# A hybrid RWKV/attention block on one core: the form of one low-rank product, the place of the state transposes, and the grouping of attention's value products

## The chip, the cores and the metric

The kernel runs on one core of one Trainium2 chip. The core has TensorE (matrix products, called PE in the profile, with its weight loads as PEld), VectorE (DVE), ScalarE (ACT), GpSimd (POOL) and SyncE (SP, which here issues DMAs). The metric is the device time of one launch in microseconds. The time before is 866.53 us, the median of three runs (866.11 to 867.91).

## What is computed

One residual block for 256 tokens of 2048 channels. The input is normalised, projected by one large matrix, run through two branches (an RWKV-7 time mixer and chunked attention, both 1024 wide with heads of 64), gated, merged, projected and normalised again. Cut to its core, the reference reads:

```python
h = _rms_norm(x, pre_norm_g[l])
proj = h @ w_in[l]
p_r, p_k, p_v, z_r, q_a, k_a_att, v_a, z_a, m_r, m_a = jnp.split(proj, split_points, axis=-1)
y_r = _rwkv7_mixer(h, p_r, p_k, p_v, ...) * jax.nn.silu(z_r)
y_a = _chunk_band_attention(q_a, k_a_att, v_a, rel_bias[l]) * jax.nn.silu(z_a)
u_r = y_r @ w_branch_rwkv[l]
u_a = y_a @ w_branch_attn[l]
merged = jax.nn.sigmoid(m_r + b_merge[l, 0]) * u_r + jax.nn.sigmoid(m_a + b_merge[l, 1]) * u_a
x = x + _rms_norm(merged @ w_out[l], post_norm_g[l])
```

In the time mixer, `a = sigmoid(a0 + (xa @ a1) @ a2)` is a low-rank product with an inner width of 64; its second layer, `@ a2`, is what the kernel calls `pa`. The state recurrence runs per head over the tokens:

```python
sa = einsum('bhvk,bhk->bhv', state, -kkt)
state = state * wt + sa * (kkt * at) + vt * kt
yt = einsum('bhvk,bhk->bhv', state, rt)
```

Attention is a softmax over the own chunk of 64 tokens and earlier ones, with a bias by relative position, followed by the product with the values.

## The kernel before

**Main products.** `run_plan` walks a list of large products (`k0`, `r0`, `v0`, the first low-rank layer, then `k`, `r`, `v`, `q`, `ak`, `zr`, `va`, `za` by column blocks, later the merge and the output). Each weight chunk is loaded by SyncE, split by ScalarE and VectorE into a high and a low part (`split`, lines 80 to 82), and multiplied in fp32r with accumulators `acc_...` in two wide PSUM buffers (pool `pm`, tag `mm`). An accumulator is free again when `done` has read it (`take`, lines 376 to 382).

**Side work.** Everything else is written as Python generators that are kept in two queues, `side` and `back`. After each chunk of a main product, `pump` takes a few steps of each: first `side`, then two of `back`. A step runs to the next `yield`. So the yields set the order in which the code asks for instructions and for buffers. The tile framework then schedules: it puts each engine's instructions in an order of its own, for which it simulates the engines, and gives out the buffers of each tag. Small results share four PSUM banks (`small`, pool `ps`, tag `sm`).

**The time mixer** handles 16 heads as eight tiles of 128 channels, two heads a tile. `duo_front(j0)` prepares two tiles (j0 is 0, 2, 4 or 6): decay sums `pc` (line 500), the low-rank `pa` (line 506), factors in `AB`, and products `pv` (546) and `pA` (553). Its 64 inner rows lie on partitions 64 to 127 of `za` and `RA`. `group_back(g)` works on four tiles (g is 0 or 1): it inverts small triangular blocks (`z`, `xx`, `x`), then runs a chain over four chunks c. In each chunk: `pw` (647, and 651 with the state `SB`), its copy `W` on ScalarE (653), the transposes `pt` (658) and their copy `BT` (659, not for the last chunk), `pu` (663) and its copies into `UV`, and after a yield `py` (672, 680), `pg` (677, from `BT` and `UV`), and the new state `SB` on VectorE (688, 690). The tag `BT` has two buffers, and `project_za` takes one of that tag for the gate `za2`.

**Attention.** `attend(j0)` handles two tiles: scores `pS` (822, 824), softmax, and then per tile the transposes `pT` of the probabilities (851) with their copies on ScalarE (853), a yield, the value products `po` (859, 862), the gate on VectorE (864) and a split into `ya`. `q`, `k` of the first two calls take buffers of the tags `k` and `r` that `duo_front` uses.

**Forms.** TensorE is addressed by rows and columns. The profile writes 128\*128 for the whole array, 64\*128 for half the rows (`pa`, `pA`, `pS`), 128\*64 for half the columns (`pv`, `pw`, `py`, `pg`, `po`), 64\*64 (`pu`, `z`, `xx`) and 32\*32. The main products, `pc`, `pt` and `pT` have the whole array. The list of buffers:

```python
pm = ctx.enter_context(tc.tile_pool(name="pm", bufs=2, space=PSUM))
ps = ctx.enter_context(tc.tile_pool(name="ps", bufs=4, space=PSUM))
```

Of the kernel before, what the change touches and what calls it, by code (L numbers as in the profile page):

```python
# [9 lines left out]
F32 = mybir.dt.float32  # L10
F32R = mybir.dt.float32r
AF = mybir.ActivationFunctionType
ALU = mybir.AluOpType
# [24 lines left out]
P = 128  # L38
D = 2048
DB = 1024  # L40
T = 256
C = 64
# [19 lines left out]
def kernel(ctx: ExitStack, tc, x, xt, vecs, w_in, wa1, w2, a2, w0, rel, w_br, w_ba, w_out, post_g, bm, out):  # L62
    nc = tc.nc
    PE, ACT, DVE, POOL = nc.tensor, nc.scalar, nc.vector, nc.gpsimd
# [4 lines left out]
    tp = ctx.enter_context(tc.tile_pool(name="tp", bufs=2))  # L69
# [4 lines left out]
    def small(name):  # L74
        return ps.tile([P, 512], F32, tag="sm", name=name)

    def col(t, o):
        return t[:, o:o + 1]
# [91 lines left out]
    ident = cp.tile([P, P], F32, name="ident")  # L170
# [193 lines left out]
    def normalise():  # L364
# [8 lines left out]
        RA.append(bg.tile([P, 2 * DB], F32, tag="R", name="RA"))  # L373
        nc.sync.dma_start(RA[0][64:128, DB:2 * DB], a2)

    def take(out, acc, raw=False):

        if raw:
            DVE.tensor_tensor(out, acc[:, :, 0:256], rb2, op=ALU.mult)
        else:  # L380
            ACT.activation(out, acc[:, :, 256:512], AF.Copy)
            DVE.tensor_tensor(out, acc[:, :, 0:256], out, op=ALU.add)
# [3 lines left out]
    RA = []  # L386
    zw = cp.tile([65, T], F32, name="zw")
    za = cp.tile([P, T], F32, name="za")
    POOL.memset(zw[64:65, :], 1.0)

    lab = []

    def lora_weights(q):
# [4 lines left out]
        else:  # L398
            lab.extend(bg.tile([P, 4, 256], F32, tag=t, name=f"lab_{t}") for t in ("Y", "s"))
        for g in (2 * q, 2 * q + 1):  # L400
# [31 lines left out]
    HS = (slice(0, 64), slice(64, 128))  # L432
# [33 lines left out]
    def duo_front(j0):  # L466
        g = j0 // 4
# [9 lines left out]
        AB, A, v, UV = d["AB"][q0 // 2], d["A"], d["v"], d["UV"]  # L477
# [19 lines left out]
        for m in range(2):  # L497
            pc = small(f"pc{j0}{m}")
            for i in range(2):
                PE.matmul(pc[:, i * 130:(i + 1) * 130], d["s"][:, i, (q0 + m) * P:(q0 + m + 1) * P],  # L500
                          cum.rearrange("p c t -> p (c t)"), start=True, stop=True)
            pcv = pc[:, 0:260].rearrange("p (c t) -> p c t", c=4)
            ACT.activation(pp[:, 4 * m:4 * m + 4, :], pcv, AF.Exp, scale=-DECAY)
            ACT.activation(iv[:, 4 * m:4 * m + 4, :], pcv[:, :, 1:65], AF.Exp, scale=DECAY)
            pa = small(f"pa{j0}{m}")
            PE.matmul(pa[:, :T], RA[0][64:128, DB + (j0 + m) * P:DB + (j0 + m + 1) * P], za[64:128, :], start=True, stop=True)
            ACT.activation(ta[:, m, :], pa[:, :T], AF.Tanh, scale=0.5, bias=col(hv, H_A0 + j0 + m))
            yield
        for m in range(2):
# [30 lines left out]
        for m in range(2):  # L540
            jj = q0 + m
# [22 lines left out]
    def group_back(g):  # L564
        d = G[g]
        AB, A, UV = d["AB"], d["A"], d["UV"]
# [17 lines left out]
        for i in range(14, -1, -1):  # L584
            n = 15 - i
# [50 lines left out]
        for q in range(2):  # L636
            ACT.activation(Rq[q][0:32, :, 32:64], p4[q][0:32, 0:256].rearrange("p (u t) -> p u t", u=8), AF.Copy)
            DVE.tensor_copy(Rq[q][64:96, :, 32:64], p4[q][64:96, 0:256].rearrange("p (u t) -> p u t", u=8))
        yield
        Y = bg.tile([P, 4, 4, C], F32, tag=("Y", "v")[g], name=f"Y{g}")  # L640
        d["Y"] = Y
        for c in range(4):
            pw = small(f"pw{g}{c}")
            for jj in range(4):
                for h in range(2):

                    PE.matmul(pw[HS[h], jj * C:(jj + 1) * C], A[:, h, jj, c, 0, :], UV[:, h, jj, c, :], start=jj == 0, stop=jj == 3 and not c)
            for jj in range(4):
                for h in range(2):
                    if c:  # L650
                        PE.matmul(pw[HS[h], jj * C:(jj + 1) * C], AB[jj // 2][:, jj % 2, c, 0, :], SB[:, jj, h, :], start=False, stop=jj == 3)
            W = tp.tile([P, 4, C], F32, tag="W", name=f"W{g}{c}", bufs=2)
            ACT.activation(W.rearrange("p j t -> p (j t)"), pw[:, 0:256], AF.Copy)
            if c < 3:
                BT = tp.tile([P, 4, P], F32, tag="BT", name=f"BT{g}{c}")
                pt = small(f"pt{g}{c}")
                for jj in range(4):
                    PE.transpose(pt[:, jj * P:(jj + 1) * P], AB[jj // 2][:, jj % 2, c, 2:4, :].rearrange("p a t -> p (a t)"), ident)
                ACT.activation(BT.rearrange("p j t -> p (j t)"), pt, AF.Copy)
            pu = small(f"pu{g}{c}")  # L660
            for jj in range(4):
                for h in range(2):
                    PE.matmul(pu[HS[h], jj * C:(jj + 1) * C], R[HS[h], jj * 4 + c, :], W[HS[h], jj, :], start=True, stop=True)
            puv = pu[:, 0:256].rearrange("p (j t) -> p j t", j=4)
            DVE.tensor_copy(UV[HS[0], 0, :, c], puv[HS[0]])
            ACT.activation(UV[HS[1], 1, :, c], puv[HS[1]], AF.Copy)
            yield
            py = small(f"py{g}{c}")
            for jj in range(4):
                for h in range(2):  # L670
                    if c:
                        PE.matmul(py[HS[h], jj * C:(jj + 1) * C], SB[:, jj, h, :], AB[jj // 2][:, jj % 2, c, 1, :], start=jj == 0, stop=False)
            if c < 3:
                pg = small(f"pg{g}{c}")
                for jj in range(4):
                    for h in range(2):
                        PE.matmul(pg[HS[h], jj * C:(jj + 1) * C], BT[:, jj, HS[h]], UV[:, h, jj, c, :], start=True, stop=True)
            for jj in range(4):
                for h in range(2):
                    PE.matmul(py[HS[h], jj * C:(jj + 1) * C], UV[:, h, jj, c, :], A[:, h, jj, c, 1, :], start=jj == 0 and not c, stop=jj == 3)  # L680
            if c < 3:
                pgv = pg[:, 0:256].rearrange("p (j t) -> p j t", j=4)
                for h in range(2):
                    fb = d["f"][HS[h], :, c].unsqueeze(2).to_broadcast([C, 4, C])
                    src = pgv[HS[h]]
                    sh = SB[HS[h], :, h, :]
                    if c:
                        DVE.tensor_tensor(sh, src, sh, op=ALU.add)
                        src = sh
                    DVE.tensor_tensor(sh, src, fb, op=ALU.mult)  # L690
            ACT.activation(Y[:, :, c, :], py[:, 0:256].rearrange("p (j t) -> p j t", j=4), AF.Copy)
            yield

        Yf = Y.rearrange("p j c t -> p j (c t)")
        for q in range(2):
# [9 lines left out]
        for q in range(2):  # L705
            for m in range(2):
                jj = 2 * q + m
                j = 4 * g + jj
# [69 lines left out]
    def gate(j0, z):  # L778
        y = G[j0 // 4]["Y"].rearrange("p j c t -> p j (c t)")[:, j0 % 4:j0 % 4 + 2, :]
        DVE.scalar_tensor_tensor(z, y, 0.5, z, op0=ALU.mult, op1=ALU.mult)  # L780
# [17 lines left out]
    va = []  # L798
# [12 lines left out]
    def attend(j0, q, k, z):  # L811
# [6 lines left out]
        for m in range(2):  # L818
            j = j0 + m
# [22 lines left out]
                    DVE.tensor_scalar_mul(S[:, h, cs], S[:, h, cs], mx[:, 2 * n + h, 2:3])  # L842
            yield
        for m in range(2):
            j = j0 + m
            S = att[0][:, 2 * m:2 * m + 2, :]
            Pt = []
            for h in range(2):
                pT = small(f"pT{j}{h}")
                for b in range(3):  # L850
                    PE.transpose(pT[:, b * P:(b + 1) * P], S[:, h, b * P:(b + 1) * P], ident)
                t = att[1][:, 2 * m + h, :]
                ACT.activation(t, pT[:, 0:384], AF.Copy)
                Pt.append(t)
            yield
            po = small(f"po{j}")
            for h in range(2):
                vc = slice((2 * j + h) * C, (2 * j + h + 1) * C)
                PE.matmul(po[HS[h], 0:256], va[0][:, vc], Pt[h][:, 0:256], start=True, stop=False)
            for h in range(2):  # L860
                vc = slice((2 * j + h) * C, (2 * j + h + 1) * C)
                PE.matmul(po[HS[h], 128:256], va[1][:, vc], Pt[h][:, 256:384], start=False, stop=True)
            yg = tp.tile([P, T], F32, tag="rn", name=f"ya{j}", bufs=1)
            DVE.scalar_tensor_tensor(yg, po[:, :T], 0.5, z[:, m, :], op0=ALU.mult, op1=ALU.mult)
            split(ya[j // 4][:, j % 4, 0, :], ya[j // 4][:, j % 4, 1, :], yg)
            yield

    tiles = {j0: {} for j0 in range(0, 8, 2)}

# [28 lines left out]
    def project_za(j0):  # L898
        def done(acc):
            if j0 < 4:  # L900
                z = tp.tile([P, 2, T], F32, tag="BT" if j0 else "zs", name=f"za{j0}", bufs=2 if j0 else 1)
            else:
                z = place(2 + j0 // 2)
            got(j0, z=z_gate(acc, f"a{j0}", z))
        project(f"za{j0}", O_ZA + j0 * P, done, quota=QB)

    later = []
    att = []
# [166 lines left out]
```

## Time and profile before

| what | value |
|---|---|
| median of three runs | 866.53 us (866.11 to 867.91) |
| the profiled execution | 866.37 us |
| its span, first to last instruction | 864.7 us |
| mean granted TensorE clock | 0.991 |
| TensorE matmul records | 5624 |

A row of the timeline has the start and the time in us, the engine, the line, the operation, output and inputs by name, the form, the count of instructions merged into the row, and in brackets the idle time of the engine before the row with what ended it. A float32 product is two records, an fp32r product is one. Records of TensorE overlap, so the time from one start to the next says more than a record's duration. In a row of the view by windows stand the stretch, its length, the busy time of each engine with its count, then the granted TensorE clock, the share of the DMA engines and GB/s.

### The profile page before, as it was taken

What the parts mean: (1) busy time and instruction counts of PE and PEld (TensorE: products, weight loads), DVE (VectorE), ACT (ScalarE), POOL (GpSimd) and SP (SyncE); (2) the same over time, 40 slices, a digit from 0 to 9 for tenths busy, and PEclk for the clock granted to TensorE, in tenths of its full rate; (3) what the DMA queues carried; (4) which work ended last, traced back from release to release, by engine and by line L of the source; (5) the groups of instructions that cost most, each with busy time, mean ns of one, the idle gap of its engine ahead of it and who ended that gap; (6) DMA issues with size and microseconds to landing.
All of it is one profiled execution on the core that took longest, in us unless ns stands there. A gap on an engine that the chain in (4) does not pass through costs nothing.

```text
span 864.7 us, 14000 instructions
## 1 busy us (share of the span) xinstructions
PE 847.0 (98%) x5624; PEld 716.0 (83%) x5624; DVE 571.4 (66%) x801; ACT 424.7 (49%) x600; POOL 16.7 (2%) x66
## 2 busy tenths in 40 slices
PE   8999999999999999999999999999999999999996
PEld 7997888888787888888887877888888888888896
DVE  6897996866759866644787864565554565555555
ACT  6567564535454444443476654434444434444433
POOL 2010000000010000000000000000000000000000
PEclk9999999999999999999999999999999999999998
DMA  9916535564134656643376445667666677676552
GB/s 284 266 50 183 177 116 154 178 173 133 54 118 146 178 155 179 197 123 120 91 236 189 129 134 167 205 193 204 205 194 193 205 206 229 214 245 203 194 190 98
DMA packets 119395, 149.35 MB, mean 173 GB/s; under 512 B 13601, under 2 KB 82209, under 8 KB 118946
## 3 DMA queue, kind: packets, MB, share of 16 engines
q1 hardware_dynamic: 105090, 138.43, 52.4%
q10 hardware_dynamic: 14240, 10.03, 4.2%
q8 instruction: 44, 0.72, 0.3%
q14 instruction: 21, 0.17, 0.1%
HBM read 145.82 MB, written 2.62 MB: 172 GB/s over the span
## 4 chain that ended last, share of the span: by engine, by line
PE 94%; DVE 2%; DMA 2%; ACT 1%; issue 1%; DVEq 0%; SPq 0%
PE acc_mr L275 10%; PE acc_ma L275 10%; PE acc_o L275 10%; PE acc_va L275 5%; PE acc_ua L275 5%; PE acc_ur L275 5%; PE acc_q L339 4%; PE acc_ak L339 4%; PE acc_zr L339 3%; PE acc_za L339 3%; PE acc_r L339 3%; PE acc_v L339 3%; PE acc_za L337 2%; PE acc_q L337 2%; PE acc_zr L337 2%; PE acc_ak L337 2%
## 5 line engine op out<-in xcount | busy, mean ns | idle before, releaser
L275 PE MATMUL acc_mr<-wh_mr,hn 128*128 128x512 f32 x256 | 80.9, 391 | 0.0
L275 PE MATMUL acc_ma<-wh_ma,hn 128*128 128x512 f32 x256 | 79.8, 390 | 0.0
L82 DVE TENSOR_TENSOR wl_ma<-raw_ma,wh_ma 128x1024 fp32r<-128x1024 f32 x32 | 39.2, 1225 | 42.7 <-ACT wh_ma L81 42.7
L82 DVE TENSOR_TENSOR wl_o<-raw_o,wh_o 128x1024 fp32r<-128x1024 f32 x31 | 37.9, 1225 | 35.0 <-ACT wh_o L81 35.0
L82 DVE TENSOR_TENSOR wl_mr<-raw_mr,wh_mr 128x1024 fp32r<-128x1024 f32 x32 | 39.2, 1224 | 30.0 <-ACT wh_mr L81 30.0
L275 PEld LDWEIGHTS acc_mr<-wh_mr,hn 128*128 128x128 f32 x256 | 48.1, 188 | 10.4 <-issue 0.7
L275 PEld LDWEIGHTS acc_ma<-wh_ma,hn 128*128 128x128 f32 x256 | 48.1, 188 | 10.3 <-issue 0.4
L81 ACT ACTIVATE wh_ma<-raw_ma 128x1024 fp32r<-128x1024 f32 x32 | 34.0, 1061 | 44.6 <-PE acc_ma L275 21.4
L81 ACT ACTIVATE wh_mr<-raw_mr 128x1024 fp32r<-128x1024 f32 x32 | 33.9, 1060 | 44.0 <-PE acc_ua L275 19.9
L81 ACT ACTIVATE wh_o<-raw_o 128x1024 fp32r<-128x1024 f32 x31 | 32.9, 1060 | 41.6 <-PE acc_o L275 25.7
L275 PE MATMUL acc_mr<-wl_mr,hn 128*128 128x512 f32 x128 | 50.1, 391 | 0.0
L275 PE MATMUL acc_ma<-wl_ma,hn 128*128 128x512 f32 x128 | 49.9, 390 | 0.0
L275 PE MATMUL acc_o<-wh_o,mgh 128*128 128x512 f32 (+1 forms) x140 | 49.9, 356 | 0.0
L275 PE MATMUL acc_o<-wl_o,mgh 128*128 128x512 f32 (+1 forms) x140 | 49.8, 356 | 0.0
L275 PE MATMUL acc_va<-wh_va,hn 128*128 128x512 f32 x128 | 40.7, 396 | 0.0
L339 PE MATMUL acc_ak<-hn,wh_ak 128*128 128x512 f32 x128 | 34.0, 400 | 0.0
L339 PE MATMUL acc_q<-hn,wh_q 128*128 128x512 f32 x128 | 33.6, 398 | 0.0
L339 PE MATMUL acc_zr<-hn,wh_zr 128*128 128x512 f32 x128 | 33.2, 396 | 0.0
L339 PE MATMUL acc_za<-hn,wh_za 128*128 128x512 f32 x128 | 32.6, 394 | 0.0
L82 DVE TENSOR_TENSOR wl_ua<-raw_ua,wh_ua 128x1024 fp32r<-128x1024 f32 x16 | 19.6, 1224 | 18.0 <-ACT wh_ua L81 18.0
L82 DVE TENSOR_TENSOR wl_ur<-raw_ur,wh_ur 128x1024 fp32r<-128x1024 f32 x16 | 19.6, 1224 | 17.9 <-ACT wh_ur L81 17.9
L82 DVE TENSOR_TENSOR wl_ak<-raw_ak,wh_ak 128x1024 fp32r<-128x1024 f32 x16 | 19.5, 1221 | 16.2 <-ACT wh_ak L81 15.1
(481 smaller groups left out, 2105.5 us busy)
## 6 DMA issues: line engine op xcount, KB each, us to landing
raw_mr<-w_in_d SPq DMA_DIRECT2D x32, 512.0 KB, 4.4
raw_ma<-w_in_d SPq DMA_DIRECT2D x32, 512.0 KB, 3.8
raw_o<-w_out_d SPq DMA_DIRECT2D x32, 512.0 KB, 4.6
raw_v<-w_in_d SPq DMA_DIRECT2D x16, 512.0 KB, 3.6
raw_q<-w_in_d SPq DMA_DIRECT2D x16, 512.0 KB, 4.1
raw_ak<-w_in_d SPq DMA_DIRECT2D x16, 512.0 KB, 3.7
raw_zr<-w_in_d SPq DMA_DIRECT2D x16, 512.0 KB, 4.0
raw_va<-w_in_d SPq DMA_DIRECT2D x16, 512.0 KB, 3.7
```

The source lines that it names most:

```text
L81: ACT.activation(h, src, AF.Copy)
L82: DVE.tensor_tensor(l, src, h.bitcast(F32), op=ALU.subtract)
L275: PE.matmul(d, u, v, start=first and n == 0, stop=last and n == len(ops) - 1)
L337: PE.matmul(acc[:, m, 0:256], wl[:, k, ms], a[:, 0, :], start=False, stop=g == ng - 1 and k == 3)
L339: PE.matmul(acc[:, m, :], wh[:, k, ms], a.rearrange("p n t -> p (n t)"), start=g == 0 and k == 0, stop=False)
```

## The change

Three edits.

The rows 0 to 63 of `za` and of the second half of `RA` are set to zero, and `pa` runs over all 128 rows instead of rows 64 to 127. The rows added contribute zero.

In `group_back`, the transposes of chunks 0 to 2 and their copies are made in one step of its own ahead of the chain, with a yield behind it. `BT` gets three buffers, also where `project_za` uses the tag.

In `attend`, the transposes of both tiles come first (a yield behind each), then the value products of both tiles in one step, then both gates and splits in one step.

```diff
+        POOL.memset(RA[0][0:64, DB:2 * DB], 0.0)
...
+    POOL.memset(za[0:64, :], 0.0)
...
-            PE.matmul(pa[:, :T], RA[0][64:128, DB + (j0 + m) * P:DB + (j0 + m + 1) * P], za[64:128, :], start=True, stop=True)
+            PE.matmul(pa[:, :T], RA[0][:, DB + (j0 + m) * P:DB + (j0 + m + 1) * P], za, start=True, stop=True)
...
+        BTs = []
+        for c in range(3):
+            BTs.append(tp.tile([P, 4, P], F32, tag="BT", name=f"BT{g}{c}", bufs=3))
+            pt = small(f"pt{g}{c}")
+            for jj in range(4):
+                PE.transpose(pt[:, jj * P:(jj + 1) * P], AB[jj // 2][:, jj % 2, c, 2:4, :].rearrange("p a t -> p (a t)"), ident)
+            ACT.activation(BTs[c].rearrange("p j t -> p (j t)"), pt, AF.Copy)
+        yield
...
-            if c < 3:
-                BT = tp.tile([P, 4, P], F32, tag="BT", name=f"BT{g}{c}")
-                pt = small(f"pt{g}{c}")
-                for jj in range(4):
-                    PE.transpose(pt[:, jj * P:(jj + 1) * P], AB[jj // 2][:, jj % 2, c, 2:4, :].rearrange("p a t -> p (a t)"), ident)
-                ACT.activation(BT.rearrange("p j t -> p (j t)"), pt, AF.Copy)
...
-                        PE.matmul(pg[HS[h], jj * C:(jj + 1) * C], BT[:, jj, HS[h]], UV[:, h, jj, c, :], start=True, stop=True)
+                        PE.matmul(pg[HS[h], jj * C:(jj + 1) * C], BTs[c][:, jj, HS[h]], UV[:, h, jj, c, :], start=True, stop=True)
...
             for h in range(2):
-                pT = small(f"pT{j}{h}")
+                pT = small(f"pT{j0 + m}{h}")
                 for b in range(3):
                     PE.transpose(pT[:, b * P:(b + 1) * P], S[:, h, b * P:(b + 1) * P], ident)
-                t = att[1][:, 2 * m + h, :]
-                ACT.activation(t, pT[:, 0:384], AF.Copy)
-                Pt.append(t)
-            yield
-            po = small(f"po{j}")
...
+                ACT.activation(att[1][:, 2 * m + h, :], pT[:, 0:384], AF.Copy)
+            yield
+        po = [small(f"po{j0 + m}") for m in range(2)]
+        for m in range(2):
+            for n, c0, c1 in ((0, 0, 256), (1, 256, 384)):
+                for h in range(2):
+                    vc = slice((2 * (j0 + m) + h) * C, (2 * (j0 + m) + h + 1) * C)
+                    PE.matmul(po[m][HS[h], 128 * n:256], va[n][:, vc], att[1][:, 2 * m + h, c0:c1], start=not n, stop=bool(n))
+        yield
+        for m in range(2):
+            j = j0 + m
             yg = tp.tile([P, T], F32, tag="rn", name=f"ya{j}", bufs=1)
-            DVE.scalar_tensor_tensor(yg, po[:, :T], 0.5, z[:, m, :], op0=ALU.mult, op1=ALU.mult)
+            DVE.scalar_tensor_tensor(yg, po[m][:, :T], 0.5, z[:, m, :], op0=ALU.mult, op1=ALU.mult)
             split(ya[j // 4][:, j % 4, 0, :], ya[j // 4][:, j % 4, 1, :], yg)
-            yield
+        yield
...
-                z = tp.tile([P, 2, T], F32, tag="BT" if j0 else "zs", name=f"za{j0}", bufs=2 if j0 else 1)
+                z = tp.tile([P, 2, T], F32, tag="BT" if j0 else "zs", name=f"za{j0}", bufs=3 if j0 else 1)
```

More of the change, by code (lines that the diff above doesn't have):

```diff
@@ L844, in attend @@
         for m in range(2):
-            j = j0 + m
             S = att[0][:, 2 * m:2 * m + 2, :]
-            Pt = []
             for h in range(2):
-                pT = small(f"pT{j}{h}")
+                pT = small(f"pT{j0 + m}{h}")
                 for b in range(3):
                     PE.transpose(pT[:, b * P:(b + 1) * P], S[:, h, b * P:(b + 1) * P], ident)
-                t = att[1][:, 2 * m + h, :]
-                ACT.activation(t, pT[:, 0:384], AF.Copy)
-                Pt.append(t)
+                ACT.activation(att[1][:, 2 * m + h, :], pT[:, 0:384], AF.Copy)
             yield
-            po = small(f"po{j}")
[L857 to L862, printed above, removed]
+        po = [small(f"po{j0 + m}") for m in range(2)]
[7 more added lines that the diff above has]
+            j = j0 + m
             yg = tp.tile([P, T], F32, tag="rn", name=f"ya{j}", bufs=1)
-            DVE.scalar_tensor_tensor(yg, po[:, :T], 0.5, z[:, m, :], op0=ALU.mult, op1=ALU.mult)
+            DVE.scalar_tensor_tensor(yg, po[m][:, :T], 0.5, z[:, m, :], op0=ALU.mult, op1=ALU.mult)
             split(ya[j // 4][:, j % 4, 0, :], ya[j // 4][:, j % 4, 1, :], yg)
-            yield
+        yield
     tiles = {j0: {} for j0 in range(0, 8, 2)}
```

## The prediction

> **What bounds the kernel now.** I read the page first: the span, the busy shares and the chain that ended last.
>
> ```profile
> span 864.7 us, 14000 instructions
> PE 847.0 (98%) x5624; PEld 716.0 (83%) x5624; DVE 571.4 (66%) x801; ACT 424.7 (49%) x600; POOL 16.7 (2%) x66
> PE 94%; DVE 2%; DMA 2%; ACT 1%; issue 1%; DVEq 0%; SPq 0%
> ```
>
> TensorE is busy for 98% of the span and carries 94% of the chain. So time taken off TensorE is time off the kernel, except where TensorE waits anyway. The change adds and drops no arithmetic that counts. What it can move is the form in which TensorE runs a product, how often it goes from one form to another, and when its few waits fall. The page gives averages, so I went to the timeline of TensorE around each edit, reading starts rather than durations, because durations of matmuls overlap.
>
> **Part 1: `pa` on all rows.** Here are, in the timeline of TensorE (start, us, engine, line, operation, tile, form, count), two of the eight `pa` products, and then a float32 product of the same 256 columns on all 128 rows (`pvr`). A float32 product shows as two records.
>
> ```profile
> 112.58 1.99 PE L339 MATMUL acc_k<-hn,wh_k 128*128 128x512 f32 x8
> 114.41 0.61 PE L500 MATMUL pc<-cum,s 128*128 128x130 f32 x4
> 114.77 1.20 PE L337 MATMUL acc_k<-hn,wl_k 128*128 128x256 f32 x8
> 115.89 0.70 PE L506 MATMUL pa<-za,RA 64*128 64x256 f32 x2
> 116.52 0.71 PE L500 MATMUL pc<-cum,s 128*128 128x130 f32 x4
> 117.17 0.70 PE L506 MATMUL pa<-za,RA 64*128 64x256 f32 x2
> 117.79 2.11 PE L339 MATMUL acc_k<-hn,wh_k 128*128 128x512 f32 x8
> 119.74 1.12 PE L337 MATMUL acc_k<-hn,wl_k 128*128 128x256 f32 x8
> 120.69 0.40 PE L339 MATMUL acc_r<-hn,wh_r 128*128 128x512 f32 x1
> ```
>
> ```profile
> 251.31 1.89 PE L700 MATMUL pvr<-ysq,onesb 128*128 128x256 f32 x8
> 253.13 0.39 PE L546 MATMUL pv<-cen,v 128*64 128x64 f32 x5
> ```
>
> From 112.58 to 120.69 are 8.11 us. Eight L339 take 1.83 (112.58 to 114.41), eight L337 take 0.95 (119.74 to 120.69); two sets of each are 5.56, which leaves 2.55 for two `pa` and two sets of four `pc` records. `pvr` gives the rate of a float32 record on all rows: 253.13 - 251.31 = 1.82 for eight, 0.228 each for 256 columns. At that rate a `pc` record of 130 columns is 0.116, and eight are 0.93. Left are 1.62, so one `pa` displaces **0.81 us**. On all rows it becomes two records like those of `pvr`, 0.46. The saving is 0.35 a product. There are four calls of `duo_front` with two products each, so 8 x 0.35 = **2.8 us**, all in stretches where TensorE has no gap. The low bound takes the bare starts of one `pa` (115.89 to 116.52, 0.63): 8 x 0.17 = 1.4.
>
> The Trainium skill, "TensorEngine Tiling (Array Packing)", Key Properties, says that changing the tiling mode drains TensorE; the bracket agrees, since the eight L339 behind the second `pa` need 1.95 where the first eight need 1.83. Its page "TensorE: Matmul & The Clock Gate", in the table of what matters for kernels, speaks against the change: a single product on 32 rows takes as long as one on 128. By that rule the 64-row records would keep their length on all rows; what that would give is the second rival below.
>
> The zeros are written by POOL: 64 x 256 elements at the start and 64 x 1024 when `RA` is made.
>
> ```profile
> 62.25 0.96 POOL L582 MEMSET RA<- 128x1024 f32 x1 [4.38 <-issue]
> ```
>
> By this row the larger one is about 1 us, on an engine that is 2% busy, beside the load of `a2` into the same tile. I cost it at nothing; without that cover it would be 1 us once, ahead of the first `pa`.
>
> **Part 2: value products of two pairs together.** The first `po` block and the last one:
>
> ```profile
> 447.01 1.77 PE L339 MATMUL acc_za<-hn,wh_za 128*128 128x512 f32 x7
> 448.71 0.65 PE L859 MATMUL po<-att_yrh,va 128*64 128x256 f32 x4
> 449.19 0.39 PE L862 MATMUL po<-att_yrh,va 128*64 128x128 f32 x4
> 449.51 0.88 PE L851 MATMUL pT<-ident,att_yrl 128*128 128x128 f32 x6
> 450.14 1.20 PE L337 MATMUL acc_za<-hn,wl_za 128*128 128x256 f32 x8
> 451.19 2.00 PE L339 MATMUL acc_za<-hn,wh_za 128*128 128x512 f32 x8
> ```
>
> ```profile
> 528.05 0.43 PE L859 MATMUL po<-att_yrh,va 128*64 128x256 f32 x1
> ```
>
> From 447.01 to 451.19 are 4.18 us. Seven L339 (7/8 of 1.83), eight L337 (0.95), six transposes of 128 columns at the `pvr` rate (6 x 0.114) and `po` with two heads side by side (two records of 256 columns and two of 128, 0.68) make 3.91. So one visit to the 128*64 form costs 0.27 beyond its work. The timeline has seven visits for `po` alone, from 448.71 to 528.05 (the first call of `attend` has one, the last has three, since `po` is split where the second head's copy is late). Three further `po` blocks run into `pS`, which has a visit anyway. The change asks for one visit a call, four: 3 x 0.27 = **0.8 us**. Low 0 (ScalarE's four copies arrive one by one and `po` is split as now), high 1.6 (all but one shared with `pS`). The number of steps of `attend` stays nine, and the work behind it is unchanged; `ya` is first read by the `ua` products, two `m` products and one `ur` product behind the last `po`.
>
> **Part 3: the state transposes ahead.** Four records, 0.4 us, six times. They cost the same at the new place. What changes is the order in which things are asked for, at two places.
>
> First place, group 0; TensorE's timeline, one row of VectorE's, and the stretch from 226 to 232 by windows, where the number ahead of the last two is the granted clock:
>
> ```profile
> 210.88 0.68 PE L663 MATMUL pu<-W,RA 64*64 64x64 f32 x16
> ...
> 216.65 0.71 PE L500 MATMUL pc<-cum,s 128*128 128x130 f32 x4
> ...
> 217.92 1.09 PE L337 MATMUL acc_ak<-hn,wl_ak 128*128 128x256 f32 x7
> ...
> 223.58 0.66 PE L658 MATMUL pt<-ident,AB 128*128 128x128 f32 x4
> 225.57 1.13 PE L651 MATMUL pw<-SB,AB 128*64 128x64 f32 x16 [1.33 <-DVE SB L690]
> 227.17 0.76 PE L663 MATMUL pu<-W,RA 64*64 64x64 f32 x16 [0.47 <-ACT W L653]
> ...
> 231.49 0.73 PE L339 MATMUL acc_zr<-hn,wh_zr 128*128 128x512 f32 x2
> ```
>
> ```profile
> 227.40 0.88 DVE L536 SCALAR_TENSOR_TENSOR r<-r,vt,k 128x256 f32<-128x256 f32 x2
> ```
>
> ```profile
> 226.00:232.00 6.00, 5.51 (x96) 5.14 (x97) 5.41 (x11) 2.86 (x6) 0.00 (x0) 0.72 0.01 3
> ```
>
> From 219.0 (`acc_ak` ends) to 231.49 TensorE has no main product: the next, `acc_zr`, needs a wide accumulator, `acc_q` holds one until `aq` takes it, and `aq` takes over the buffer of `k` of `duo_front(4)`, free only after L536 (228.3). TensorE idles 1.33 + 0.47 = 1.8 us, and behind that the granted clock is 0.72 for 6 us (1.7 us of work): about 3.5 us lost. Two transposes run inside this hole at no price; ahead of it they lie among main products and cost 0.9.
>
> Against that, the extra yield shifts the chain by one step. A pump runs two steps of `duo_front` and then two of the chain. Before, the code asks for small PSUM banks (four in all) in the order first `pc`/`pa`, all of chunk 0, second `pc`/`pa`; after it, second `pc`/`pa` stand ahead of chunk 0's `py` and `pg`. If banks are handed out in the order of the code, the second `pc`, now at 216.65 behind `py`, can run right after `pu` (210.88). I put it at 213.3: 0.6 for `pu`, and 1.8 later for three transpose copies on ScalarE ahead of `W` (0.60 each, by the `BT` row below). L536 and `acc_zr` then come some 3 us sooner, near 228 and less; the main products end near 220 instead of 219.0; the chain has some 4 to 5 us of work in that gap, so about 2.8 us stay lost. I take a gain of **0.7**, bounds -2 (the hidden transposes and their cover lost) and 3.5 (the hole closes).
>
> Second place, group 1, on TensorE, ScalarE and TensorE again:
>
> ```profile
> 353.80 1.21 PE L337 MATMUL acc_za<-hn,wl_za 128*128 128x256 f32 x8
> ```
>
> ```profile
> 388.08 0.60 ACT L659 ACTIVATE BT<-pt 128x512 f32<-128x512 f32 x1 [0.67 <-PE pt L658]
> 388.57 0.59 ACT L381 ACTIVATE za<-acc_za 128x512 f32<-128x512 f32 x1
> ```
>
> ```profile
> 389.98 0.68 PE L663 MATMUL pu<-W,RA 64*64 64x64 f32 x16 [0.73 <-ACT W L653]
> ```
>
> `acc_za` is complete at 355 and is taken only at 388.57, right after the third `BT`: `za2` shares that tag, two buffers, and stands behind all three `BT` in the code. This is the evidence that buffers go out in the order of the code. With three buffers `za2` waits only for the first `BT`, which `pg` of chunk 0 reads; now it waits for the second, a chunk later. The wide accumulator is free a chunk of the chain sooner, and the wait of 0.73 with no main product at 389.98 should go: **0.7**, low 0.
>
> The sum: 2.8 + 0.8 + 0.7 + 0.7 = 5.0. The profiled execution took 866.37 (864.7 of span and 1.7 around it), which the median of 866.53 matches: 866.5 - 5.0 = **861.5 us**.
>
> **Rivals.**
> - *The hole at 219 to 231 widens* (C). `acc_zr` does not come sooner, and the pulled transposes leave only idle behind: part 3 gives -2 and 0 instead of 1.4, in all 1.6, 864.9. For: DVE is busy nearly throughout that hole. Against: its start hangs on `pc` at 216.65.
> - *Row count does not matter* (B). A `pa` keeps its 0.32 a record and saves only the two changes of form, 0.81 - 0.64 = 0.17: 1.4 in place of 2.8, 862.9. Against: `pvr` and `pc` stream at 0.228 and 0.116.
> - *The hole closes* (D): 3.5 instead of 0.7, 858.7.
> - *Slower* (E). Three transposes occupy three of the four small banks, each until ScalarE's copy, and `pw` of chunk 0, `pu` and so the second `pc` queue behind them. Each us by which that `pc` starts after 216.65 delays `k`'s release, `acc_zr` and the end by one. With 4.3 gained elsewhere it turns slower by over 1.7 us from a start near 222.7 on; at 225 it would be 870.6. Against: ScalarE needs 1.8 us for the copies, not 8.
>
> **How the numbers follow.** About 0.2% (1.7 us) is what a measurement of this kernel can tell from no change. Chances: the forecast 0.56, B 0.10, D 0.12, all three faster, 0.78. C 0.14, within 0.2%. E 0.08, slower. The range 858.5 to 865.2 leaves out E and the tails of C and D, below 2 in 10.
>
> **What would show it.** Right: `pa` as 128*128, start to next start about 0.43 to 0.46 and no slow row behind it; four to five `po` blocks; the second `pc` of `duo_front(4)` ahead of chunk 0's `pg`; `za2` taken right behind chunk 0's `pg`; no idle at 225 or 390. Wrong: `pa` still 0.32 a record; `po` blocks as many as now; idle of TensorE above 2.7 us between 200 and 400; or a new gap in the attention, where both `po` now hold banks until VectorE reads them one after the other. It would fail as a whole if the scheduler placed the chain elsewhere among the main products and left a hole that this trace does not have.

## The result, and the profile after

The changed kernel takes 873.16 us (median of six runs, 871.46 to 876.31), the kernel before 866.32 beside it (six runs). The ratio is 1.0082, 95% interval 1.0059 to 1.0104. The prediction was 861.5, with 858.5 to 865.2 as its range. The change makes the kernel slower by about 7 us. Of the runs below, two had one slow execution each (1190.61 us with the yield alone, 1669.22 with three buffers for `BT` and `za2`), and their times are the medians of the others.

The page of the kernel after (span; busy time, share and records of each engine):

```profile
span 871.6 us, 13996 instructions
PE 846.0 (97%) x5624; PEld 716.5 (82%) x5624; DVE 572.0 (66%) x801; ACT 424.5 (49%) x600; POOL 17.3 (2%) x68
```

TensorE is busy for 1.0 us less than before (846.0 against 847.0) in a span that is 6.9 longer. So against the kernel before the difference is waiting. To find where, here is the view by windows, before and then after. A row has the stretch, its length, and the busy time of PE, PEld, DVE, ACT and POOL, each with its count; the granted clock, the DMA share and GB/s end it.

```profile
218.00:226.00 8.00, 6.57 (x129) 5.58 (x129) 7.51 (x17) 2.84 (x7) 0.00 (x0) 1.00 0.24 75
226.00:234.00 8.00, 7.51 (x107) 6.84 (x108) 6.24 (x12) 3.22 (x7) 0.00 (x0) 0.79 0.01 2
360.00:430.00 70.00, 69.27 (x708) 58.02 (x707) 37.40 (x52) 30.75 (x44) 0.00 (x0) 1.00 0.36 112
```

```profile
218.00:226.00 8.00, 6.67 (x97) 6.06 (x98) 7.31 (x16) 2.60 (x6) 0.00 (x0) 0.57 0.17 60
226.00:234.00 8.00, 8.00 (x56) 6.58 (x55) 3.25 (x4) 2.77 (x4) 0.00 (x0) 1.00 0.22 66
360.00:430.00 70.00, 62.22 (x825) 52.80 (x826) 35.05 (x48) 27.34 (x43) 0.00 (x0) 1.00 0.38 122
```

From 360 to 430 TensorE waits 0.73 us before and 7.78 after. These 7.05 us are as much as the whole difference in time, and they lie in group 1, not in the stretch around 219 that the prediction priced. They are not all that the change loses, since parts 1 and 2 by themselves gain 5.4 us, as an experiment below shows. Four of the waits there (TensorE's timeline, kernel after); two more are 1.39 us ahead of `xx` at 364.55 and 0.47 ahead of `pu` at 422.05:

```profile
368.35 2.14 PE L339 MATMUL acc_ak<-hn,wh_ak 128*128 128x512 f32 x8 [1.52 <-DVE aq L384]
386.62 2.12 PE L339 MATMUL acc_q<-hn,wh_q 128*128 128x512 f32 x8 [1.49 <-DVE ak L384]
420.45 1.13 PE L662 MATMUL pw<-SB,AB 128*64 128x64 f32 x16 [1.02 <-DVE SB L695]
423.25 1.09 PE L685 MATMUL py<-A,UV 128*64 128x64 f32 x16
426.03 2.11 PE L339 MATMUL acc_q<-hn,wh_q 128*128 128x512 f32 x8 [1.69 <-DVE late L384]
```

The last row is the clearest. `acc_q` of pair 6 needs a wide accumulator; both are held, by `acc_q` and `acc_ak` of pair 4, whose results go into the tile `late`. That tile takes over the buffer of `A` (tag A, one buffer), and `A` is read to the end by the last `py` of group 1's chain, at 423.25. Before, that chain is through before `acc_ak` of pair 4 is complete, and the two takes are far apart. The rows of VectorE, after and then before:

```profile
425.28 0.69 DVE L384 TENSOR_TENSOR late<-acc_q,late 128x512 f32<-128x512 f32 x1 [2.08 <-ACT late L383]
425.89 0.68 DVE L384 TENSOR_TENSOR late<-acc_ak,late 128x512 f32<-128x512 f32 x1
```

```profile
411.92 0.68 DVE L382 TENSOR_TENSOR late<-acc_q,late 128x512 f32<-128x512 f32 x1
430.85 0.68 DVE L382 TENSOR_TENSOR late<-acc_ak,late 128x512 f32<-128x512 f32 x1
```

Why is group 1's chain late? Follow it back: it needs group 1's `A`, and `A` is written late. The last writing of it, after and then before (VectorE, two instructions a row):

```profile
316.71 1.28 DVE L559 TENSOR_TENSOR A<-pA,msk 128x512 f32<-128x512 f32 x2
```

```profile
306.57 1.29 DVE L556 TENSOR_TENSOR A<-pA,msk 128x512 f32<-128x512 f32 x2
```

And that is late since group 0's chain is late. Group 0's last `py` ends at 257.1 after and at 245.3 before, and the first writing of group 1's `A` starts 15.8 and 15.2 us behind it. On VectorE it stands behind a closing step of group 0, which needs that last `py` too (kernel after):

```profile
265.46 6.59 DVE L715 RECIPROCAL rs<-rs 128x256 f32<-128x256 f32 x4 [0.78 <-ACT rs L707]
...
272.88 0.68 DVE L559 TENSOR_TENSOR A<-pA,msk 128x512 f32<-128x512 f32 x1
```

Group 0's `A` and group 1's share one buffer, which also has to be read to the end first; the memsets below show whether that is what holds. TensorE in group 0, after:

```profile
211.81 0.71 PE L503 MATMUL pc<-cum,s 128*128 128x130 f32 x4
...
220.84 1.12 PE L668 MATMUL pu<-W,RA 64*64 64x64 f32 x16 [0.47 <-ACT W L664]
...
225.77 2.11 PE L339 MATMUL acc_zr<-hn,wh_zr 128*128 128x512 f32 x8
...
234.23 0.68 PE L668 MATMUL pu<-W,RA 64*64 64x64 f32 x16
...
250.43 0.68 PE L668 MATMUL pu<-W,RA 64*64 64x64 f32 x16
...
256.45 0.68 PE L685 MATMUL py<-A,UV 128*64 128x64 f32 x14
```

and before, where chunk 2's `pu` at 227.17 and `acc_zr` at 231.49 lie between these rows:

```profile
220.61 0.68 PE L663 MATMUL pu<-W,RA 64*64 64x64 f32 x16
...
239.94 0.68 PE L663 MATMUL pu<-W,RA 64*64 64x64 f32 x16
...
244.62 0.69 PE L680 MATMUL py<-A,UV 128*64 128x64 f32 x16
```

The second `pc` came early, as forecast (211.81), and so did `acc_zr` (225.77). But read the `pu` of chunks 1, 2 and 3. Before: 220.61, 227.17, 239.94. After: 220.84, 234.23, 250.43. From one `pu` to the next, a chunk that runs while TensorE has no main product takes 6.6 us; one that runs among main products takes 12.8 to 16.2, as its dependent steps come behind some three to five us of them. (From chunk 0 to chunk 1, partly among main products, it is 9.7 in both kernels.) Before, `acc_zr` starts behind chunk 2's `pu`; after, ahead of it.

The start-up of the kernel differs by a few us between the profiled executions, one for each kernel, and the part from the first `acc_ur` to the end is 317.5 or 317.6 in every one. So below, beside the times, I use **D**, the time from the first `acc_q` (pair 0) to the first `acc_ur` product in the timeline: 364.2 before (182.91 to 547.11), 374.0 after (180.03 to 554.02). On the same ruler group 0's last `py` stands at 61.7 before and 76.4 after, the end of the last writing of `A` at 125.0 and 138.0. `acc_zr` starts 2.9 us sooner (48.6 before, 45.7 after), and the chain starts 3.1 us later, behind the twelve records of the transposes put ahead: `pw` of chunk 0 stands at 23.3 before and at 26.4 after, `pu` of chunk 1 at 37.7 and 40.8.

### The profile page after: what moved, and what is told of

Same layout as the page of the kernel before. It is cut to its first block, busy times and chain, and to the rows that moved or that the text cites. A ratio compares the mean times of both kernels' runs of the same rounds, so it can differ in the third digit from the quotient of the medians.

```text
span 871.6 us, 13996 instructions
## 1 busy us (share of the span) xinstructions
PE 846.0 (97%) x5624; PEld 716.5 (82%) x5624; DVE 572.0 (66%) x801; ACT 424.5 (49%) x600; POOL 17.3 (2%) x68
## 4 chain that ended last, share of the span: by engine, by line
PE 54%; DVE 1%; ACT 0%; DVEq 0%; issue 0%
PE acc_mr L275 10%; PE acc_ma L275 10%; PE acc_o L275 9%; PE acc_ua L275 5%; PE acc_ur L275 5%; PE acc_q L339 2%; PE acc_za L339 2%; PE acc_ak L339 2%; PE acc_q L337 1%; PE acc_za L337 1%; PE acc_ak L337 1%; PE acc_zr L339 1%; PE po L862 1%; PE acc_last L275 1%; PE pT L854 1%; PE pS L829 1%
## 5 line engine op out<-in xcount | busy, mean ns | idle before, releaser
L81 ACT ACTIVATE wh_ak<-raw_ak 128x1024 fp32r<-128x1024 f32 x16 | 16.7, 1056 | 31.5 <-PE acc_q L339 13.9
```

The source lines that it names most:

```text
L81: ACT.activation(h, src, AF.Copy)
```

## The experiments

The times of the first four runs stand beside 865.45 us for the kernel before, measured with them, those of the next four beside 865.49; for the runs with four and seven memsets it is 865.96, for nine 866.01, for the last run 865.84.

**Which part loses.** Theory Y: the added yield moves group 0's chain against the main products. Rival P: any gain on TensorE in front of it does.

*Part 1 alone.*

```diff
-            PE.matmul(pa[:, :T], RA[0][64:128, ...], za[64:128, :], start=True, stop=True)
+            PE.matmul(pa[:, :T], RA[0][:, ...], za, start=True, stop=True)
```

> Before with part 1 alone (pa on all rows). Theory Y (the extra yield re-orders the chain of group 0, group 1 comes late, and that makes the loss): 863, that is 3.2 below before, eight times the 0.4 by which two pa shift the start of acc_r in the trace of the changed kernel. Rival P (any time won on TensorE lets the chain of group 0 come late, whichever edit wins it): 870 or more, with acc_zr starting early and the last py of group 0 near 256.

862.35 us, ratio 0.9968 (0.9952 to 0.9985); D 362.8, last `py` of group 0 at 61.1 on the ruler. P falls: the gain stays a gain.

*The yield alone*, put into the kernel before, ahead of the chain.

```diff
         yield
+        yield
         Y = bg.tile([P, 4, 4, C], F32, tag=("Y", "v")[g], name=f"Y{g}")
```

> Before with nothing but one more yield ahead of the chain in group_back. Theory Y: the second pc of duo_front(4) comes ahead of chunk 0's pg, the last py of group 0 moves from 245 to about 256, z of group 1 from 346 to about 359, and the time is 5 to 9 above before: 871 to 875. Rivals T (the pulled transposes make the loss) and A (the attention part does): 866, as before.

872.31 us, ratio 1.0070 (1.0053 to 1.0086); D 370.0. One added `yield`, which issues nothing, costs 6.9 us. Its TensorE rows show the pattern of the kernel after: `acc_zr`, then chunk 2's `pu`, the last `py` of group 0, and the wait for `late`.

```profile
226.93 2.25 PE L339 MATMUL acc_zr<-hn,wh_zr 128*128 128x512 f32 x8
...
234.60 0.68 PE L664 MATMUL pu<-W,RA 64*64 64x64 f32 x16
...
256.11 0.69 PE L681 MATMUL py<-A,UV 128*64 128x64 f32 x16
...
422.89 2.12 PE L339 MATMUL acc_q<-hn,wh_q 128*128 128x512 f32 x8 [1.70 <-DVE late L382]
```

*The change without the yield.*

```diff
             ACT.activation(BTs[c].rearrange("p j t -> p (j t)"), pt, AF.Copy)
-        yield
         Y = bg.tile([P, 4, 4, C], F32, tag=("Y", "v")[g], name=f"Y{g}")
```

> The changed kernel without the extra yield: the transposes are still ahead of the chain, in one step with chunk 0's pw and pu. Theory Y: the order of pc, py and pg is that of before, the last py of group 0 comes near 245, no hole at 417 to 426, 862 to 864. Rival T (the pulled transposes): 871 to 875 as the changed kernel. Rival A (attention): the same 871 to 875.

871.35 us, ratio 1.0067 (1.0045 to 1.0088); D 371.7. Y is wrong here: the transposes put ahead lose nearly as much without any yield. So the yield is one way to the loss and not the cause. The rows gave a first idea why: all twelve records of `pt` stand in front of `pw` of chunk 0, which comes at 206.33 and not, as with part 1 alone, at 203.1.

```profile
202.85 1.47 PE L648 MATMUL pt<-ident,AB 128*128 128x128 f32 x12
...
206.33 0.69 PE L657 MATMUL pw<-UV,A 128*64 128x64 f32 x16
...
232.50 0.68 PE L667 MATMUL pu<-W,RA 64*64 64x64 f32 x16
...
252.73 0.69 PE L684 MATMUL py<-A,UV 128*64 128x64 f32 x16
```

*More main work in group 1.* If the wait at 426 were only a lack of something to run, another main product in front of it should fill it.

```diff
-ORDER = "q0 r2 v0 z0 v1 r6 r0 z2 q2 q4 q6 z4 r4 z6"
+ORDER = "q0 r2 v0 z0 v1 r6 r0 z2 q2 r4 q4 q6 z4 z6"
```

> The changed kernel with zr4 moved ahead of q4 and ak4 in the list of products: 11 us of main products that need nothing of the late tile of tag A. Theory Y, its last link (acc_q of q4 and acc_ak hold both wide accumulators until A of group 1 is free): the hole of some 8 us between 417 and 426 goes, of which 3 to 7 us come back: 866 to 870. If the hole is owed to something else than the wait for A: 872 to 874.

871.4 us, ratio 1.0063 (1.0046 to 1.0080); D 372.2. The gain is smaller than Y expected (866 to 870), and the time lies below the other range too. The wait moved:

```profile
435.74 3.48 PE L339 MATMUL acc_q<-hn,wh_q 128*128 128x512 f32 x8 [1.70 <-DVE late L384]
```

Chunk 3's `pu` of group 1 went from 422.05 to 429.58: with more main products the chain spreads over them, as it seems, like that of group 0.

**Theory Q.** From here the theory was: what counts is whether group 0's chunk 2 stands ahead of `acc_zr` or behind it; whatever shifts it behind (a yield, transposes) makes group 0's chain end late, the single buffer of `A` hands that on to group 1, and there it becomes waits. Four runs to test it.

*Parts 1 and 2 without part 3* (their edits as in the change).

> Before with parts 1 and 2 alone (low-rank a on all rows; attention's value products of two pairs together); no transposes pulled ahead, no extra yield. TensorE's queue holds both chains of state where it does in the run with part 1 alone. Theory Q (the loss of the whole change lies in where group 0's chain stands against the next wide product, and the other parts leave that alone): 860.8 to 862.4, that is part 1's 862.35 less 0 to 1.6, as the forecast priced part 2; last py of group 0 at 240.7 and z of group 1 at 341.6, both within 0.5. Rival R (part 2 takes a share of the loss): over 864.

860.07 us (858.7 to 860.77), ratio 0.9931 (0.9910 to 0.9952); D 361.0. This is faster than both kernels. Last `py` and `z` came at 239.45 and 340.3, each 1.3 us earlier than with part 1 alone, as did the first `acc_q`; so the place of the chain is the same. Rivals A and R, that part 2 takes a share of the loss, fall.

*The same with three buffers for `BT` and `za2`.*

```diff
-                BT = tp.tile([P, 4, P], F32, tag="BT", name=f"BT{g}{c}")
+                BT = tp.tile([P, 4, P], F32, tag="BT", name=f"BT{g}{c}", bufs=3)
...
-                z = tp.tile(..., name=f"za{j0}", bufs=2 if j0 else 1)
+                z = tp.tile(..., name=f"za{j0}", bufs=3 if j0 else 1)
```

> Before with parts 1 and 2, and the tag BT with three buffers for the transposes and za2, as the change has it, the transposes left in their chunks. Theory Q: acc_za2 is taken sooner (before: 389.98, behind the last transposes of group 1; now some 3 us sooner in its own kernel), the chain's order stays, and the time is 860 to 862.4: the forecast gave this place 0.7. Rival R2 (the third buffer sends za2's gate and the attention steps between the chain's, and group 1's chain or the late accumulators lose by it): over 864.

859.32 us, the same ratio 0.9931; D 360.9. The time was as expected, but not the reason: `acc_za2` is not taken sooner. ScalarE's timeline:

```profile
384.37 0.60 ACT L662 ACTIVATE BT<-pt 128x512 f32<-128x512 f32 x1 [0.67 <-PE pt L661]
384.87 0.59 ACT L383 ACTIVATE za<-acc_za 128x512 f32<-128x512 f32 x1
```

The take still stands right behind the third `BT`. A free buffer did not help it; its place behind the third transposes did not change. What puts it there is not shown.

*The transposes behind `pw` of chunk 0* (change without the yield).

```diff
             ACT.activation(W.rearrange("p j t -> p (j t)"), pw[:, 0:256], AF.Copy)
+            if not c:
+                BTs = []
+                for e in range(3):
+                    BTs.append(tp.tile([P, 4, P], F32, tag="BT", name=f"BT{g}{e}", bufs=3))
...
```

> After without the extra yield, and with the three transposes of a group put behind the first chunk's pw and W instead of ahead of them, so that pw of chunk 0 goes where it does before (203). Theory Q: what counts is the place of chunk 2's pu against acc_zr of the group; in this kernel's TensorE queue it still stands behind the first wide chunk of acc_zr, so last py of group 0 stays over 250, z of group 1 over 350 and the time is 867 to 873. Rival S (the loss without the yield comes from pw of chunk 0 standing behind three transposes, 203.1 to 206.3): with pw of chunk 0 back in place the time is 861 to 863.5.

871.64 us, ratio 1.0067 (1.0043 to 1.0091); D 371.0. `pw` of chunk 0 is back at 203.64, and nothing is gained, so rival S falls. Chunk 2's `pu` still comes behind `acc_zr`, as Q asks:

```profile
203.64 0.68 PE L650 MATMUL pw<-UV,A 128*64 128x64 f32 x16
...
226.84 3.78 PE L339 MATMUL acc_zr<-hn,wh_zr 128*128 128x512 f32 x8 [0.33 <-DVE aq L384]
...
232.57 0.68 PE L668 MATMUL pu<-W,RA 64*64 64x64 f32 x16
...
254.38 0.69 PE L685 MATMUL py<-A,UV 128*64 128x64 f32 x16
```

*The whole change, with `acc_zr` held back* until chunk 2 is through.

```diff
             ACT.activation(UV[HS[1], 1, :, c], puv[HS[1]], AF.Copy)
+            if (g, c) == (0, 2):
+                DVE.tensor_copy(mark, UV[0:64, 0, 0, 2, 0:1])
...
+                if not j0:
+                    DVE.tensor_copy(t[0:64, 0, 0:1], mark)
                 take(t, acc)
```

> The change whole, with the yield, and one wait added: the takes of acc_q and acc_ak of pair 0 wait (by one 64x1 copy each) for group 0's chunk 2 UV, so that no wide accumulator comes free for acc_zr until chunk 2 is through, as it came about by itself in before. Theory Q (the loss is group 0's chain cut apart by acc_zr, carried to group 1 by the single buffer of A): pu of chunk 2 at 222 to 227, ahead of acc_zr, last py of group 0 at 240 to 244, z of group 1 at 341 to 347, and the time 862 to 867 although TensorE is held idle some 3 us longer at 219 to 230. Rival R3 (the loss comes from the later steps themselves, such as the yield in group 1 or the attention's order): the added wait costs its idle time on top, 873 to 877.

867.79 us, ratio 1.0016 (0.9999 to 1.0032); D 367.5. A wait was added and 5.4 us were won. Rival R3 falls. The time lies 0.8 above the range that Q gave, and the last `py` is still 3.3 us later on the ruler (65.0) than before.

```profile
227.67 0.68 PE L669 MATMUL pu<-W,RA 64*64 64x64 f32 x16 [0.53 <-ACT W L665]
...
230.62 2.14 PE L339 MATMUL acc_zr<-hn,wh_zr 128*128 128x512 f32 x8
...
244.22 0.68 PE L688 MATMUL py<-A,UV 128*64 128x64 f32 x14
```

**The link through `A`, by itself.** Now parts 1 and 2 with group 0's chain left as it was, and only the handing over of `A` delayed, in three doses (n is 4, 7 and 9).

```diff
             for h in range(2):
                 POOL.memset(d["UV"][HS[h], h], 0.0)
+            if g:
+                for _ in range(n):
+                    POOL.memset(d["A"], 0.0)
```

> Parts 1 and 2 alone (860.07), and group 1's A written over with zeros by GpSimd four times ahead of its first use, which keeps A from group 1 for some 15 us (four times a memset of 128x4096; 128x1024 took 0.95) behind group 0's last py at 239.4. Group 0's chain is left compact. A<-pA ran at 255.3, so this takes the slack of the link and about 2 us more. Theory Q: N of group 1 (307.4) and its z (340.3) come 0 to 3 us later, TensorE's order in group 1 stays, time 859.5 to 862. Rival T (what costs the change its time is group 0's chain itself, cut apart among acc_zr and acc_va): the same, 860.

> As the run with four memsets, with seven: A comes to group 1 some 26 us behind group 0's last py, as late as (in the kernel after) 266 to 269 us. Group 0's chain is still compact and ends at 239.4. Theory Q (the loss comes about in group 1, by the late release of A): N of group 1 at 316 to 322, z of group 1 at 350 to 356, both late accumulators held until the chain of group 1 is through, and the time 866 to 872, most of the change's loss with none of its edits to the chain. Rival T (group 0's cut chain itself costs it): 860 to 862, as with four.

> As the run with seven memsets, with nine. With seven, the last writing of group 1's A came 129.8 us behind the start of acc_q of pair 0 (parts 1 and 2 alone 123.5, the kernel after 137.4), only 6.3 of after's 13.9 us, and the time was 3.7 over parts 1 and 2 alone. Each memset took 3.57, so nine add some 7 us: last writing of A at 135 to 138, N, z and the chain of group 1 later by as much; in TensorE's queue group 1's chain then stands against acc_ak, acc_q and acc_ak of the later pairs as it does in the run of the extra yield alone. Theory Q (the late release makes the loss, by steps as the chain of group 1 slides into the wide products whose accumulators it holds): 866 to 871, that is the 872.35 of the extra yield alone less the 5.4 of parts 1 and 2, within 3. Rival T2 (the release carries only what the run with seven showed, the rest is group 0's cut chain): 863 to 865.

| memsets | last writing of `A` on the ruler | D | time, us | ratio to before |
|---|---|---|---|---|
| none | 123.5 | 361.0 | 860.07 | 0.9931 (0.9910 to 0.9952) |
| 4 | 124.0 | 361.5 | 862.28 | 0.9956 (0.9939 to 0.9974) |
| 7 | 129.9 | 364.1 | 863.76 | 0.9988 (0.9966 to 1.0009) |
| 9 | 137.4 | 366.5 | 868.05 | 1.0025 (1.0005 to 1.0044) |
| (the change) | 138.0 | 374.0 | 873.16 | 1.0082 (1.0059 to 1.0104) |

Four keep the buffer for 16 us behind group 0's last `py` (it starts at 242.02, they end at 259.10) and move the last writing of `A` by 0.5 us. So the buffer has slack, and it is not what passes group 0's delay on to `A` in the changed kernel, where it is also free for 15.8 us before the first writing. That something does is plain: in all eleven kernels without memsets the last writing of `A` ends 60.8 to 63.3 us behind the start of group 0's last `py`. Whether it is VectorE's order, with group 0's closing steps ahead of `A`, or the buffer of `UV`, which the last `py` frees too, no run separates. The memsets delay `A` by another way and so test only what a late `A` does from there on.

With four the time lies 0.3 above the range expected, and the medians differ by 2.2 from none, D by 0.5. With seven I had expected 866 to 872: they delay `A` by 6.4 us and not by the 13 or so that I had taken, and cost 3.1 in D. Nine delay it nearly as much as the change does, and two of the waits of the kernel after come back, though group 0's chain is compact and nothing else of part 3 is there (from 360 to 430 TensorE waits 3.94 us, 7.78 in the kernel after):

```profile
242.57 32.17 POOL L482 MEMSET A<- 128x4096 f32 x9
```

```profile
364.02 2.11 PE L339 MATMUL acc_ak<-hn,wh_ak 128*128 128x512 f32 x8 [1.56 <-DVE aq L384]
...
417.84 2.11 PE L339 MATMUL acc_q<-hn,wh_q 128*128 128x512 f32 x8 [1.70 <-DVE late L384]
```

So this link is shown: a late `A` alone costs 5.5 in D, 8.0 by the medians; against four memsets, which are work of the same kind, 5.0 and 5.8. The memsets do not slow VectorE: the splits `wl_va` beside them take 1.22 us each, as without them. A late `A` is not the whole loss of 13.0 against parts 1 and 2. The rival that puts all of it on the cut chain falls, and so does the strict form of Q, that the late `A` makes the whole loss.

*Part 3 in group 1 alone.*

```diff
         BTs = []
-        for c in range(3):
-            BTs.append(...)
+        if g:
+            for c in range(3):
+                BTs.append(...)
...
+            yield
...
+            if not g and c < 3:
+                BTs.append(...)
```

> The change whole, but the transposes ahead of the chain and the yield for group 1 alone; group 0 keeps its transposes in the chunks and has no added yield. Against parts 1 and 2 alone (860.07) the change loses 13.1, of which the late release of A by itself made 8.0 (the run with nine memsets). This run has no late release: group 0's chain stands as in parts 1 and 2, its last py at 239 to 241, z of group 1 at 340 to 343. Theory Q2 (the other 5.1 comes about in group 1, whose own chain is cut by the yield and the pulled transposes): 864 to 867. Theory Q3 (group 1's cut alone costs only what the run that held acc_zr showed behind group 0, about 2 to 3; the rest of the 5.1 comes from group 0's cut chain: form switches and half clock there): 861 to 863.9.

862.61 us, ratio 0.9964 (0.9947 to 0.9980); D 362.4. This is Q3's range: in group 1 part 3 costs 1.4 in D, 2.5 by the medians. Rival Q2 (864 to 867) falls. Here, with the transposes pulled, `acc_za2` is taken early (369.71, right behind chunk 0's `pg`), and the wait ahead of `pu` that the prediction wanted gone is gone. A new one stands in its place; TensorE and ScalarE:

```profile
368.30 0.33 PE L689 MATMUL pg<-UV,BT 128*64 128x64 f32 x2 [1.28 <-DVE UV L677]
```

```profile
369.71 0.60 ACT L383 ACTIVATE za<-acc_za 128x512 f32<-128x512 f32 x1 [1.05 <-PE pg L689]
```

What is settled and what is open. Of the 13.0 us of D between the change and parts 1 and 2, the late `A` alone makes 5.5 and part 3 in group 1 alone 1.4. About 6 are left, if such parts may be added. The run that held `acc_zr` back also has a later `A` (127.9) and still loses 6.5 of the 13.0. The view by windows over the stretch of D tells waiting from busy time: TensorE is idle for 3.6 us with parts 1 and 2, 6.7 with nine memsets and 11.0 in the change, and busy for 357.4, 359.8 and 363.0. So against parts 1 and 2 the 13.0 are 7.4 of waiting and 5.6 of longer busy time for the same products. In the kernel after, the granted clock is 0.57 from 218 to 226, where parts 1 and 2 have 1.00; that is at most 3.4 us of TensorE time (8 x 0.43). The rest could be changes of form among the cut chain, and what part 3 does in group 1 when `A` is late as well. No run takes these apart.

## Why the prediction was wrong

**What bounds the kernel.** Right as far as it went: time taken off TensorE is time off the kernel. Part 1 and part 2 show it.

**Part 1 (2.8).** Right, slightly low. With part 1 alone the kernel gains 3.1. The same stretch as in the prediction, with the same products in it, went from 8.11 to 7.33 us (110.48 to 117.81), 0.39 a product against 0.35 forecast:

```profile
110.48 1.99 PE L339 MATMUL acc_k<-hn,wh_k 128*128 128x512 f32 x8
...
113.70 0.60 PE L509 MATMUL pa<-za,RA 128*128 128x256 f32 x2
...
114.58 0.60 PE L509 MATMUL pa<-za,RA 128*128 128x256 f32 x2
...
117.81 2.00 PE L339 MATMUL acc_r<-hn,wh_r 128*128 128x512 f32 x8
```

Rival B, that only the changes of form would be saved (0.17 a product), falls. The rule of the Trainium skill in "TensorE: Matmul & The Clock Gate" that B stood beside, that a single product on 32 rows takes as long as one on 128, does not carry to this float32 product on 64 rows.

**Part 2 (0.8, at most 1.6).** The gain was there and larger, 2.3 by the medians and 1.8 in D. The step that it rested on, one visit a call, did not happen. The value products of the two tiles do not stand together: in parts 1 and 2 the blocks of the first call start at 442.25 and 445.00 with 1.9 us of `acc_za` between them. `po` still begins ten times, where it began twelve times. What part 2 removed is two splits. With part 1 alone four of the eight blocks are split: two of a block's eight records run ahead and take 0.57 us (449.15 to 449.72), and the six behind take 0.79 (450.58 to 451.37), as much as a whole block of eight (0.80, 445.00 to 445.80 with parts 1 and 2). With part 2 two blocks are split, so two splits are saved, about 1.1 us. The term was mis-sized because its 0.27 was read from a block that is not split (448.71); what makes up the rest of the 1.8 is open.

**Part 3, first place (0.7, between -2 and 3.5).** This is where it failed. Its first half came true: the second `pc` moved ahead of chunk 0's `pg` (211.81; on the ruler 31.8, where it was 33.7 before and 30.4 forecast), and `acc_zr` came sooner, at 45.7 on the ruler against 48.6, by the 3 us that were forecast. The step that failed is the next: "the chain has some 4 to 5 us of work in that gap, so about 2.8 us stay lost". It priced the gap as lost TensorE time only, and took the chain behind it as it stood. But the gap was what let chunks 1 and 2 run back to back. With `acc_zr` 2.9 us sooner and the chain's start 3.1 us later, chunk 2's `pu` fell behind it and went from 6.6 to 13.4 us after chunk 1's, chunk 3 from 12.8 to 16.2, and the last `py` from 61.7 to 76.4 on the ruler. Then `A` came 13.0 us later; a delay of 13.9 by itself, with nine memsets, cost 5.5 in D. The prediction followed none of this to group 1, although `A`, `UV` and `late` stood in the code it read. The bounds covered the gap and not what hung on it. The two starts alone do not decide the order: with the transposes behind `pw` of chunk 0, `pu` of chunk 1 is at 37.6 on the ruler and `acc_zr` at 46.0, and chunk 2's `pu` still comes behind it. Why the scheduler chooses so is open. The 1.7 us that the prediction counted for the clock are not seen as time either: with a stretch at 0.50 in the gap (parts 1 and 2 with three buffers) and without one (parts 1 and 2) D is 360.9 and 361.0.

**Part 3, second place (0.7, low 0).** Nothing of it was seen. A third buffer by itself does not bring `za2` forward, so the place of `acc_za`'s take behind the third `BT` was no evidence for the order of buffers. With pulled transposes it comes forward, and in place of the wait of 0.73 stands one of 1.28 for `UV`, a step earlier in the same chain. The prediction named a stall that goes, and not what is late next.

**The rivals.** C and D spoke of the size of the gap in group 0, where the matter was not decided. E ended on the right side by a mechanism that did not occur: its sign was a second `pc` later than 222.7, and it came at 211.81. Its 0.08 was the whole chance of slower. The last sentence of the prediction, that the scheduler might place the chain elsewhere among the main products and leave a hole that was not there, is what happened; it had neither a price nor a chance of its own. The price could have been read from the trace of before: a chunk took 6.6 us in the gap and 12.8 behind it.

## What to carry to other kernels

A gap of the busiest engine can be the time in which a chain of dependent steps catches up. Before closing one, read how long a link of that chain takes inside the gap and outside it, follow the chain's end to the buffers and the engines that it frees, and see who needs them next. And where a framework orders the queues, a step that issues nothing can cost more than the work one saves: change one part at a time, and keep those that leave the order alone, which here were parts 1 and 2.

## What the runs showed of the hardware

The clock after short waits is not the same each time. The kernel with parts 1 and 2 has the same order and the same waits of 1.33 and 0.47 us in group 0 as the kernel before (and two shorter ones behind them, 0.31 and 0.19). Its rows by windows:

```profile
218.00:226.00 8.00, 5.57 (x130) 4.64 (x125) 7.33 (x16) 3.46 (x7) 0.00 (x0) 1.00 0.14 52
226.00:234.00 8.00, 8.00 (x65) 6.67 (x62) 4.17 (x7) 2.89 (x4) 0.00 (x0) 1.00 0.24 67
```

The granted clock stays at 1.00 behind them, where the kernel before fell to 0.79 from 226 to 234: it has 0.50 there from 228 to 231. Eight of the profiled executions have this order and these waits (the second is 0.47 to 0.53); the clock fell in four of them, before, three buffers, seven memsets and part 3 in group 1 alone, and not in the other four. With waits of 2.16 and 0.47 the kernel after has 0.57 from 218 to 226. The Trainium skill, "TensorE: Matmul & The Clock Gate", What's actually happening, gives an idle window of about 3.4 us for the fall to half rate. Single waits in these rows are shorter than that and the clock still fell in some executions; whether shorter waits within one window add up is not shown here.
